# The order of gather jobs in a decoder step: the keys of tile 8 interleaved with the second half of tile 0's values, the keys of tile 5 with the values of tile 8

## The chip, the cores and the metric

The kernel runs on one core of a Trainium2 chip. The metric is the device time of one execution in microseconds (us). The engines are named as in the profile: PE (matmul), PEld (the weight load of a matmul), DVE, ACT, POOL and SP. DMAs are issued from the queues of SP, ACT and POOL.

## The reference, cut to what matters

One decoder layer is computed for 1024 prompt positions and 64 sample positions: a gating and a retention block with a common input and output projection, a cross-attention, and a mixer that picks single-neuron experts. The change touches only the mixer:

```python
def block(xt):                                   # 128 positions
    q = (xt @ wq).reshape(PEER_BLOCK, PEER_HEADS, 2, PEER_DHALF)
    s = jnp.einsum('thcd,hckd->thck', q, subkeys).astype(jnp.float32)
    sv, si = lax.top_k(s, PEER_TOPK)
    ...
    eidx = jnp.take_along_axis(cidx, fi, axis=-1)      # 8 heads x 16 experts a position
    g = jax.nn.softmax(fv, axis=-1).astype(xt.dtype)
    act = jax.nn.gelu(jnp.einsum('thed,td->the', u_tab[eidx], xt))
    return jnp.einsum('the,thed->td', g * act, v_tab[eidx])
```

`u_tab` holds the experts' keys and `v_tab` their values, 16384 rows of 1024 numbers each. A position needs 128 rows of either.

## The kernel before, in words

The 1088 positions are nine tiles: 0 to 7 of 128 rows, and tile 8, the 64 sample rows. They pass through the projections in four batches ([0], [1, 2, 8], [3, 4, 5], [6, 7]). The generator `front` emits this work: the matmuls with streamed weights (line 148), and behind each of them the small steps of the tile. The last steps of a tile are in `post_peer`: scores (lines 602 to 611), two top-k stages on DVE (617 to 642), and the expert numbers by one-hot products (648 to 668), in which POOL does the product of line 660. What comes out is called the selection of the tile here.

The mixer has two ways. Tiles 1 to 4 (`DT`) take the dense way: the selection is turned into a dense matrix of weights by one-hot matmuls (lines 691 to 723; line 691 starts a tile, line 719 is the bulk, one tile at a time), and after `front` the generator `dense` multiplies with all 16384 experts: line 973 with the keys, line 1024 with the values. Tiles 0, 8, 5, 6 and 7 (`GT`) take the gather way, emitted by the generator `gathers`. A gather job fetches 128 rows, 512 KB, by one indirect DMA that POOL issues:

- a `u` job (keys, line 1154) ends in a dot product on DVE (line 1087, called a dot below; two rows in an order or two records in the trace, the second reads the sum out);
- a `v` job (values, line 1157) ends in four narrow matmuls on PE (line 1128; two column halves, each two records in the trace); they are issued for four `v` jobs together, when the fourth has landed, so up to three landed `v` jobs hold their buffers;
- a `w` job (values of tile 7, line 1154 too) ends in a multiply-add on DVE (line 1099).

All jobs share `NG` = 7 buffers `gbuf`, and use a job three jobs after its gather. The jobs stand in one list, made at lines 880 to 892 from `JORD`: parts in one string, parted by a blank, are interleaved by their lengths; "a" and "b" are the halves of a part. A job whose tile has no selection yet holds up the whole list (line 1145). Which instruction of the two generators comes first on an engine is decided at build time by priorities (lines 1163 to 1176, one job costs 1.1 or 1.4 units) and a scheduler; on the chip each engine runs its own list in order.

Of the kernel before, what the change touches and what calls it, by code (L numbers as in the profile page):

```python
# [68 lines left out]
ND = 2  # L69
GT = [0,8,5,6,7]  # L70
DT = [1,2,3,4]
JORD = ("u0","v0","u8","v8","u5","v5a","u6 v5b","u7 v6","w7")
FB = 2
COST_G = 1.4
COST_F = 1.1
# [83 lines left out]
def body(ctx: ExitStack, tc: tile.TileContext, a):  # L159
# [720 lines left out]
    jobs = []  # L880
    for grp in JORD:
        parts = []
# [355 lines left out]
```

## Time and profile before

| | us |
|---|---|
| median of 3 executions | 3674.6 |
| lowest, highest | 3663.38, 3684.58 |
| the profiled execution | 3672.27 |
| its span, first to last instruction | 3670.5 |

The profile is of one execution. A table of stretches gives the busy time of each engine between two times from the span's start, with the count of records behind it, then the granted PE clock as a share of 2.4 GHz, the busy share of the 16 DMA engines and their GB/s. A row of a table of waits reads: the waiting engine, tile and line, what it waited for, total us, times, longest. The profile has 40 slices, each of 91.8 us.

### The profile page before, as it was taken

How to read it: one execution, taken by the hardware profiler on the slowest of the kernel's cores; microseconds unless marked ns; L12 is line 12 of the kernel's file. 1: busy time of each engine (PE TensorE's matmuls, PEld its weight loads, DVE VectorE, ACT ScalarE, POOL GpSimd, SP SyncE). 2: the span in 40 equal slices, each digit the busy share in tenths (PEclk: the TensorE clock that was granted, in tenths of full speed). 3: DMA queues.
4: the chain of work that ended last, by engine and by line, in shares of the span. 5: the costliest groups of instructions: out<-in, count | busy, mean ns of one | idle time of the engine just before them, and what ended most of it. 6: DMA issues, size and time to landing. Idle time of an engine off the chain costs nothing.

```text
span 3670.5 us, 41634 instructions
## 1 busy us (share of the span) xinstructions
PE 3244.9 (88%) x13368; PEld 2037.7 (56%) x13368; DVE 2496.5 (68%) x5941; ACT 1274.3 (35%) x2634; POOL 1784.9 (49%) x1427
## 2 busy tenths in 40 slices
PE   8999558889997899984789779999999999999998
PEld 3444223333445554442445467777777777788886
DVE  2135874325678622799858769878877777799996
ACT  1121211112238785231677932222322322322222
POOL 0013575234546633446744546555565655566631
PEclk9989679899998899986889889999999999999999
DMA  8747677778768887667888879988999989898872
GB/s 271 258 158 275 214 285 278 253 268 283 269 235 330 309 307 283 210 235 263 300 308 313 305 275 338 327 306 316 337 332 347 343 317 324 298 322 318 309 239 75
DMA packets 407354, 1039.67 MB, mean 283 GB/s; under 512 B 37280, under 2 KB 129632, under 8 KB 403040
## 3 DMA queue, kind: packets, MB, share of 16 engines
q0 software_dynamic: 165888, 604.05, 45.3%
q1 hardware_dynamic: 229392, 420.06, 33.5%
q10 hardware_dynamic: 11856, 12.91, 1.0%
q8 instruction: 105, 1.72, 0.2%
q14 instruction: 113, 0.93, 0.1%
HBM read 985.59 MB, written 51.25 MB: 282 GB/s over the span
## 4 chain that ended last, share of the span: by engine, by line
PE 63%; DVE 13%; DMA 9%; POOL 5%; issue 5%; ACT 5%; SPq 0%; POOLq 0%; DVEq 0%; ACTq 0%
PE mm L148 20%; PE h L973 15%; PE cb L1128 5%; PE oa L1024 4%; PE oc L1024 4%; PE od L1024 4%; PE ob L1024 4%; DVE gbuf L1087 4%; DMA gbuf<-in_U_dram,ix 3%; POOL gbuf L1154 2%; PE gb L719 2%; DMA gbuf<-in_V_dram,ixT 2%; DMA ret<-in_cv_dram 1%; ACT oj L702 1%; ACT oj L703 1%
## 5 line engine op out<-in xcount | busy, mean ns | idle before, releaser
L148 PE MATMUL mm<-wr,aT 128*128 128x512 f32 (+1 forms) x2432 | 1126.5, 611 | 34.2 <-DMA aT<-in_xpT_dram 19.0
L1154 POOL DMA_INDIRECT gbuf<-in_U_dram,ix x576 | 711.8, 1236 | 540.7 <-DVE hd L1087 340.2
L1087 DVE CUSTOM_DVE_ANT_0 gbuf<-gbuf,x2g 128x1024 f32<-128x1024 f32 x576 | 733.6, 1287 | 239.7 <-DMA gbuf<-in_U_dram,ix 207.2
L1157 POOL DMA_INDIRECT gbuf<-in_V_dram,ixT x448 | 493.8, 1102 | 568.7 <-PE cb L1128 323.9
L148 PEld LDWEIGHTS mm<-wr,aT 128*128 128x128 f32 (+1 forms) x2432 | 439.2, 190 | 586.0 <-issue 524.2
L973 PE MATMUL h<-x,uh 128*128 128x512 f32 x2048 | 644.3, 392 | 0.8 <-ACT uh L917 0.8
L973 PEld LDWEIGHTS h<-x,uh 128*128 128x128 f32 x2048 | 385.8, 189 | 91.9 <-issue 6.7
L973 PE MATMUL h<-x,ul 128*128 128x512 f32 x1024 | 401.6, 392 | 3.3 <-DVE ul L918 3.3
L917 ACT ACTIVATE vh<-vr 128x1024 fp32r<-128x1024 f32 x128 | 134.9, 1061 | 491.4 <-PE od L1024 487.6
L1128 PE MATMUL cb<-gbuf,Z 128*32 128x512 f32 x1792 | 242.8, 636 | 20.4 <-DMA gbuf<-in_V_dram,ixT 20.3
L1154 POOL DMA_INDIRECT gbuf<-in_V_dram,ix x128 | 182.4, 1425 | 123.6 <-DVE fo L1099 97.8
L917 ACT ACTIVATE ah<-ga 128x512 fp32r<-128x512 f32 x128 | 80.8, 632 | 454.4 <-DVE ga L980 438.7
L719 PE MATMUL gb<-oi,oj 128*128 128x128 f32 x1024 | 168.8, 312 | 68.7 <-ACT big L720 37.9
L918 POOL TENSOR_TENSOR vl<-vr,vh 128x1024 fp32r<-128x1024 f32 x64 | 159.9, 2499 | 130.6 <-ACT vh L917 91.5
L719 PEld LDWEIGHTS gb<-oi,oj 128*128 128x128 f32 x1024 | 151.7, 218 | 127.0 <-ACT oj L703 43.7
L973 PEld LDWEIGHTS h<-x,ul 128*128 128x128 f32 x1024 | 193.0, 188 | 50.0 <-issue 5.0
L703 ACT ACTIVATE oj<-oj,kt 128x128 f32<-128x128 f32 x512 | 215.0, 483 | 0.0
L1099 DVE SCALAR_TENSOR_TENSOR fo<-gbuf,hd,fo 128x1024 f32<-128x1024 f32 x127 | 184.9, 1456 | 1.2
L917 ACT ACTIVATE uh<-ur 128x1024 fp32r<-128x1024 f32 x128 | 134.8, 1054 | 122.5 <-PE h L973 115.7
L705 DVE TENSOR_TENSOR oi<-cst,kt 128x512 f32<-128x512 f32 x128 | 88.9, 700 | 129.4 <-PE gb L719 128.0
L660 POOL TENSOR_TENSOR cd<-cd,sif 128x512 f32<-128x512 f32 (+1 forms) x72 | 105.5, 1478 | 144.4 <-DVE cd L658 134.0
L918 DVE TENSOR_TENSOR ul<-ur,uh 128x1024 fp32r<-128x1024 f32 x128 | 161.8, 1264 | 14.8 <-ACT uh L917 14.7
(232 smaller groups left out, 5102.1 us busy)
## 6 DMA issues: line engine op xcount, KB each, us to landing
ur<-in_Ud_dram SPq DMA_DIRECT2D x128, 512.0 KB, 7.0
vr<-in_V_dram SPq DMA_DIRECT2D x128, 512.0 KB, 5.8
wr<-in_w_in_dram SPq DMA_DIRECT2D x192, 256.0 KB, 5.2
wr<-in_pq_dram SPq DMA_DIRECT2D x128, 256.0 KB, 5.4
gsc<-big SPq DMA_DIRECT2D x32, 1024.0 KB, 6.9
G<-gsc SPq DMA_DIRECT2D x32, 1024.0 KB, 17.9
wr<-in_w_o_dram SPq DMA_DIRECT2D x64, 256.0 KB, 4.9
wr<-in_wq_dram SPq DMA_DIRECT2D x64, 256.0 KB, 6.4
```

The source lines that it names most:

```text
L148: self.nc.tensor.matmul(p, lhsT=lT(k), rhs=w, start=k == 0, stop=k == KB - 1)
L703: nc.scalar.activation(oj[:, r % 4, :], oj[:, r % 4, :], AF.Relu, bias=kt[:, 2, r:r + 1], scale=kt[:, 4, r:r + 1])
L719: nc.tensor.matmul(g4[:, r * 128:(r + 1) * 128], lhsT=oj[:, r, :], rhs=oi[:, r, :], start=True, stop=True)
L917: nc.scalar.activation(hi, raw, AF.Copy)
L918: eng.tensor_tensor(lo, raw, hi.bitcast(F32), op=ALU.subtract)
L973: nc.tensor.matmul(p, lhsT=w[:, k, :], rhs=x[:, k, :], start=k == 0 and j == 0, stop=k == 7 and j == 2)
L1024: nc.tensor.matmul(o[j], lhsT=A[i][ia][:, n * 128:(n + 1) * 128], rhs=Vw[i][iv][:, j * 512:(j + 1) * 512], start=b == 0 and ia + iv == 0, ...
L1087: dot = nc.vector.tensor_tensor_reduce(out=g, in0=g, in1=x2s[t], scale=1.0, scalar=0.0, op0=ALU.mult, op1=ALU.add, accum_out=hd[t][:, i:i ...
L1099: dot = nc.vector.scalar_tensor_tensor(fo[t], g, hd[t][:, i:i + 1], fo[t], op0=ALU.mult, op1=ALU.add)
L1128: nc.tensor.matmul(comb[t][q:q + 32, :], lhsT=Z[:, z + 4 * c1 + r1 % 4, 31 - r1:63 - r1], rhs=g1[:, n * 512:(n + 1) * 512], start=r1 == VQ ...
L1154: nc.gpsimd.indirect_dma_start(out=g, out_offset=None, in_=a["U" if kind == "u" else "V"], in_offset=bass.IndirectOffsetOnAxis(ap=done["ix ...
L1157: nc.gpsimd.indirect_dma_start(out=g, out_offset=None, in_=a["V"], in_offset=bass.IndirectOffsetOnAxis(ap=done["ixT", t][:, i:i + 1], axis=0))
```

## The change

One line is changed. It orders the gather jobs; nothing is computed in another way, and the number of jobs is the same.

```diff
-JORD = ("u0","v0","u8","v8","u5","v5a","u6 v5b","u7 v6","w7")
+JORD = ("u0","v0a","u8 v0b","u5 v8","v5a","u6 v5b","u7 v6","w7")
```

Before, the list has 64 more `v` jobs of tile 0 ahead of the first job of tile 8, and all 64 `v` jobs of tile 8 ahead of the first of tile 5. Now the 64 second `v` jobs of tile 0 alternate with the 64 `u` jobs of tile 8, and of the 128 `u` jobs of tile 5 two go with one `v` job of tile 8. From "v5a" on the list is the same.

**POOL, ahead of tile 8's first gather.** These rows stand where the selections of tiles 1, 2 and 8 are worked out; `cd` is the one-hot product of line 660, `mv` the norm statistics. Before:

```order
L1157 DMA gbuf<-in_V_dram,ixT 128x1024 x7
L660 TENSOR_TENSOR cd<-cd,sif 128x512 x2
L1157 DMA gbuf<-in_V_dram,ixT 128x1024 x4
L660 TENSOR_TENSOR cd<-cd,sif 128x512 x2
L283 TENSOR_TENSOR mv_g<-mv_g,mhalf 128x1 x2
```

After:

```order
L1157 DMA gbuf<-in_V_dram,ixT 128x1024
L283 TENSOR_TENSOR mv_g<-mv_g,mhalf 128x1 x4
L283 TENSOR_TENSOR mv_r<-mv_r,mhalf 128x1 x2
L660 TENSOR_TENSOR cd<-cd,sif 128x512 x2
L283 TENSOR_TENSOR mv_g<-mv_g,mhalf 128x1 x2
L660 TENSOR_TENSOR cd<-cd,sif 128x512 x2
L660 TENSOR_TENSOR cd<-cd,sif 64x512 x2
```

The gathers of tile 0's second half have left this place; they come after the selection of tile 8.

**DVE, in the work on the 14th selection part of the dense tiles (tiles 3 and 4), which goes on beside tile 5's jobs.** `abf` and `ab` belong to the selection. Before:

```order
L650 CAST abf_10143<-ab_10138 128x128
L1087 ISA gbuf_10135,hd_9323<-gbuf_10135,x2g_9249 128x1024
L1087 ISA hd_9323 128x1
L393 TENSOR_TENSOR on_10986<-on_10986,gl_10431 128x128
L1087 ISA gbuf_10186,hd_9323<-gbuf_10186,x2g_9249 128x1024
L1087 ISA hd_9323 128x1
L1087 ISA gbuf_10219,hd_9323<-gbuf_10219,x2g_9249 128x1024
L1087 ISA hd_9323 128x1
L651 SCALAR_TENSOR_TENSOR abf_10143<-abf_10143 128x32
```

After:

```order
L1121 COPY Z_135<-wT_9056 128x8
L341 TENSOR_TENSOR ret_10537<-ret_10537,rt_10542 128x2x64 x2
L650 CAST abf_9874<-ab_9869 128x128
L651 SCALAR_TENSOR_TENSOR abf_9874<-abf_9874 128x32
L1087 ISA gbuf_9917,hd_9029<-gbuf_9917,x2g_8952 128x1024
L1087 ISA hd_9029 128x1
L652 SCALAR_TENSOR_TENSOR abf_9874<-abf_9874 128x32
```

Fewer dots stand between two steps of the selection.

**PE, just ahead of the first one-hot matmul of tile 3.** `nat` are transposes of a normed tile, `mm` the projections. Before:

```order
L296 MATMUL sm<-cst,nat 128x128 x3
L148 MATMUL mm<-wr,aT 128x512 x5
L296 MATMUL sm<-cst,nat 128x128
L148 MATMUL mm<-wr,aT 128x512 x19
L691 MATMUL gb<-cst,eid 128x128 x2
```

After:

```order
L1128 MATMUL cb<-gbuf,Z 32x512 x8
L296 MATMUL sm<-cst,nat 128x128 x4
L148 MATMUL mm<-wr,aT 128x512 x22
L1128 MATMUL cb<-gbuf,Z 32x512 x8
L148 MATMUL mm<-wr,aT 128x512 x6
L691 MATMUL gb<-cst,eid 128x128 x2
```

Groups of eight narrow matmuls of tile 8's `v` jobs now stand among the projections.

Counted over the whole lists: ahead of the first one-hot matmul of tile 3, DVE has 76 dots of tile 5 before and 57 after, and 27 other instructions fewer. When the selections of tiles 6 and 7 are done (the second pair of line 729), PE has behind it 520 narrow matmuls of line 1128 before and 456 after, of 896, with the same 96 of line 973; DVE has done 12 dots of tile 6 before, and none after. The last `w` step stands on DVE where PE's list has 2825 of 3072 matmuls of line 1024 before, and 2976 after.

## Rows read from the trace of the kernel before

**Rows 1.** The profile's page: busy time of the engines, and three lines of the table of 40 slices (tenths).

```profile
PE 3244.9 (88%) x13368; PEld 2037.7 (56%) x13368; DVE 2496.5 (68%) x5941; ACT 1274.3 (35%) x2634; POOL 1784.9 (49%) x1427
...
PE   8999558889997899984789779999999999999998
...
DVE  2135874325678622799858769878877777799996
...
PEclk9989679899998899986889889999999999999999
```

**Rows 2.** Busy time by stretch, all engines: start and end, length, then busy us (records) of PE, PEld, DVE, ACT and POOL, granted clock, DMA share, GB/s.

```profile
900.00:1110.00 210.00, 197.20 (x809) 87.52 (x801) 146.97 (x754) 72.54 (x191) 108.44 (x107) 0.98 0.73 251
1110.00:1450.00 340.00, 298.99 (x1364) 176.11 (x1365) 171.93 (x322) 268.49 (x654) 172.47 (x150) 0.91 0.88 325
1450.00:1520.00 70.00, 70.00 (x219) 33.64 (x218) 43.73 (x228) 20.20 (x53) 8.49 (x9) 1.00 0.43 128
1520.00:1760.00 240.00, 150.16 (x459) 80.40 (x458) 222.43 (x831) 54.42 (x140) 138.27 (x117) 0.78 0.72 252
1760.00:2130.00 370.00, 300.79 (x1391) 183.21 (x1391) 255.71 (x828) 290.73 (x729) 191.07 (x160) 0.88 0.84 305
2570.00:3190.00 620.00, 613.71 (x2888) 454.23 (x2887) 468.68 (x706) 164.36 (x209) 361.19 (x285) 1.00 0.91 327
3190.00:3550.00 360.00, 360.00 (x1565) 293.71 (x1564) 356.27 (x411) 107.80 (x136) 219.99 (x143) 1.00 0.89 313
```

**Rows 3.** Busy time by stretch of line 1128 alone (PE, PEld), the narrow matmuls of the `v` jobs.

```profile
900.00:1110.00 210.00, 38.23 (x300) 7.96 (x292) 0.98 0.73 251
2570.00:3190.00 620.00, 65.18 (x528) 14.01 (x528) 1.00 0.91 327
```

**Rows 4.** Waits in the stretch 900 to 1110 us: the longest of POOL, and the first of the selection's chain.

```profile
POOL gbuf L1157 <- PE cb L1128: 56.5, 16, 8.9
...
ACT sif L626 <- DVE si L622: 24.7, 6, 6.0
```

**Rows 5.** The first gathers of tile 8 on POOL, from the timeline (start us, us).

```profile
1114.48 1.01 POOL L1154 DMA_INDIRECT gbuf<-in_U_dram,ix  x1 [4.71 <-DMA ix<-ix]
```

**Rows 6.** Busy time by stretch of line 1087 alone (DVE), the dots.

```profile
1520.00:1760.00 240.00, 97.82 (x153) 0.78 0.72 252
```

**Rows 7.** The timeline of PE around the start of tile 3's one-hot matmuls, and at the end of tile 4's (start us, us; in brackets the idle time before, and what ended it).

```profile
1753.61 0.69 PE L691 MATMUL gb<-cst,eid 128*128 128x128 f32 x2 [25.96 <-DVE eid L664]
...
2125.69 2.75 PE L719 MATMUL gb<-oi,oj 128*128 128x128 f32 x10 [1.04 <-ACT oj L703]
```

**Rows 8.** Waits of DVE for the gathers of keys, and the gathers of keys issued (count, us to landing): first the stretch 1520 to 1870 us, in which tile 5's `u` jobs run alone, then 2210 to 2570 us, in which `u6` and `v5b` run two to one.

```profile
DVE gbuf L1087 <- DMA gbuf<-in_U_dram,ix: 13.8, 10, 5.4
...
gbuf<-in_U_dram,ix POOLq DMA_INDIRECT x128, 6.7
...
DVE gbuf L1087 <- DMA gbuf<-in_U_dram,ix: 46.9, 33, 6.0
...
gbuf<-in_U_dram,ix POOLq DMA_INDIRECT x96, 7.4
```

**Rows 9.** The longest wait of POOL in the stretch 1760 to 2130 us.

```profile
POOL gbuf L1157 <- PE cb L1128: 77.3, 17, 12.5
```

**Rows 10.** DVE at the end of the `w` jobs and tile 7's last steps, from the timeline (start us, us).

```profile
3552.61 2.59 DVE L1099 SCALAR_TENSOR_TENSOR fo<-gbuf,hd,fo 128x1024 f32<-128x1024 f32 x2
3555.24 1.23 DVE L1070 SCALAR_TENSOR_TENSOR gbuf<-gbuf,fo 128x1024 f32<-128x1024 f32 x1
3556.50 1.28 DVE L276 BATCH_NORM_STATS2 bn_y<-gbuf 128x6 f32<-128x512 f32 x2
...
3565.39 1.23 DVE L898 TENSOR_TENSOR gbuf<-gbuf 128x1024 f32<-128x1024 f32 x1 [0.44 <-ACT gbuf L288]
...
3567.66 1.22 DVE L899 TENSOR_TENSOR gbuf<-gbuf 128x1024 f32<-128x1024 f32 x1
```

**Rows 11.** Busy time by stretch of POOL's gather issues alone: line 1157 in the first row, line 1154 in the other two.

```profile
900.00:1110.00 210.00, 68.42 (x69) 0.98 0.73 251
...
1520.00:1760.00 240.00, 98.97 (x82) 0.78 0.72 252
...
3190.00:3550.00 360.00, 179.17 (x126) 1.00 0.89 313
```

**Rows 12.** The last matmul of PE, from the timeline (start us, us).

```profile
3652.52 0.40 PE L1024 MATMUL od<-vh,al 128*128 128x512 f32 x1
```

## The prediction, made before the changed kernel ran

> **What bounds the kernel now.** I read the page first, then busy time by stretch, then the waits and the timeline inside the stretches that the change touches. From slice 24 on (2,200 us) PE is busy nine tenths or more nearly everywhere [rows 1]: the dense part is bound by PE, and whatever PE has to do there costs its full time. Before that PE has holes. The stretches show them [rows 2]. In 900 to 1110 us (tile 0's second half of `v` jobs) PE is busy 197.2 of 210 us. In 1110 to 1450 us (`u8`, then `v8`) it stands still for 41 of 340 us. In 1520 to 1760 us (tile 5's `u` jobs) PE is busy only 150.2 of 240 us, while DVE has 222.4: there DVE sets the pace, and PE then waits 26 us for a selection on DVE [rows 7]. In 1760 to 2130 us PE, ACT and DVE have 301, 291 and 256 of 370 us, and none is full. So the question for the change is where PE's `v` work goes (out of a stretch full on PE, or into one), and how many dots stand ahead of the selections on DVE.
>
> **The change part by part.** All work stays the same in sum; I follow PE's and DVE's lists from stretch to stretch. Gains are negative.
>
> *900 to 1110 us: 64 `v` jobs leave.* In the changed list nothing of the gathers is left here but the end of "v0a". A job is four records of line 1128, and a record takes 38.23 / 300 = 0.127 us [rows 3], so 64 x 4 x 0.127 = 32.6 us of PE. PE is busy 94% here, so I take 0.94 x 32.6 = -30.6. POOL also loses the waits for these buffers, 56.5 us [rows 4], behind which the selection's product of line 660 stood. What is late next: tile 8's first gather still waits for its selection [rows 5], a chain over DVE, ACT and POOL, and DVE is 147 of 210 us busy [rows 2]. If that chain sets the end of the stretch, the gain is 0; so the bounds are -33 and 0.
>
> *1110 to 1450 us: the same 64 `u` and 64 `v` jobs, mixed.* The `v` jobs are now tile 0's. Before, DVE is loaded in the first half and PE in the second; mixed, PE's 41 us of standing still could fall to the share of the stretch before (6%): 299 / 0.94 = 318, or -22. Nothing shows how much of the idle time came from the dots, so I take half, -11, with bounds -22 and +11.
>
> *1450 to 1520 us* has no gather in either list: 0.
>
> *1520 to 1760 us: `u5` with `v8`.* Up to the first one-hot matmul of tile 3, DVE has 57 dots in place of 76, and 27 other instructions fewer. A dot takes 97.82 / 76.5 = 1.28 us (two records each) [rows 6]; the others (222.43 - 97.82) / (831 - 153) = 0.18 us [rows 2, 6]. That is 19 x 1.28 + 27 x 0.18 = 29.3 us less on the engine that sets the pace: -29.3. PE takes up some 28 `v` jobs, 28 x 4 x 0.127 = 14 us, in its 90 us of idle time: 0. But each dot now depends on a queue that PE can hold up. Up to three `v` jobs hold their buffers until the fourth lands, so a gather of keys starts later, and DVE, in order, waits for it with the selection behind. The row that is nearest is the stretch in which `u6` and `v5b` run two to one: 46.9 us of waits for 96 dots, 0.49 us a dot, against 13.8 / 128 = 0.11 with `u5` alone [rows 8]. The difference over 57 dots is 57 x 0.38 = +21.7. The bounds are 0 (the dots there come 0.7 as often, with more time for each) and the price of the slower rival below, +73.
>
> *1760 to 2130 us: one-hot matmuls of tiles 3 and 4, the last projections.* The lists of both kernels have the same 256 one-hot matmuls, the same projections and nearly the same `v` jobs between these two points, 136 narrow matmuls before and 144 after; 71 dots of tile 5 stand here in place of 52, but the 12 of tile 6 have left. I take 0, with bounds of 15 to either side.
>
> *Dense part: more `v` work in it.* At the same place of the lists PE is 64 narrow matmuls behind (520 against 456), which are 32 jobs. They are paid where PE is full, at 65.18 / 132 = 0.494 us a job [rows 3]: +15.8. Without that the gain in 900 to 1110 us would be counted twice.
>
> *The end.* The list's end comes later against PE's: after the last `w` step 96 matmuls of line 1024 are left, where 247 were. 360 us of `w` jobs with DVE at 99% [rows 2] move along with PE and slow it no more than before. Tile 7's last steps, 1.23 + 1.28 + 1.23 + 1.22 = 5.0 us on DVE [rows 10], now fall among PE's last accumulations: +5, with bounds 0 and +15 (DVE late by several steps as well).
>
> The sum is -30.6 - 11 - 29.3 + 21.7 + 15.8 + 5 = -28.4. Against the profiled execution, 3672.3 us with a span of 3670.5, that gives 3643.9. The median of the three executions is 2.3 us above the profiled one, so I put the forecast at 3646 us, 0.8% faster.
>
> **The rivals.**
>
> *Larger gain.* Dots find their gathers landed (DMA engines are 72% busy in 1520 to 1760 us, and 90% where I took the wait from), mixing gives all of the 22 us, and the end costs nothing: -30.6 - 22 - 29.3 + 15.8 = -66, or 3608 us. For it: DVE waited only 10 times for `u5`'s gathers [rows 8]. Against it: there were seven free buffers then.
>
> *No change.* PE's 30.6 us in 900 to 1110 us don't come back, since tile 8's selection sets the end of the stretch: 3646 + 31 = 3677 us. For it: ACT waits 24.7 us for the top-k on DVE there [rows 4], so the chain is not far behind. Against it: PE was 94% busy.
>
> *Slower.* In 1520 to 1760 us buffers of `v` jobs come free only when PE gets to their narrow matmuls, and PE's list has these behind transposes and projections that themselves wait for DVE. POOL then waits, and gathers of keys, line 660 and the norms queue behind it. POOL's waits for line 1128 cost 77.3 / 17 = 4.5 us each where `v` jobs stand among one-hot work [rows 9]; 16 groups of four `v8` jobs make 73 us in place of my 21.7, and mixing gives nothing: 3646 + 51 + 11 = 3708 us. It turns the sign when DVE's waits for gathers of keys, from the first `u5` job to tile 3's first one-hot matmul, pass some 50 us. For it: PE stood still for 90 us there, each time behind something. Against it: with PE so free, a narrow matmul seldom has other matmuls ahead of it.
>
> *POOL's issue blocked.* An issue takes 0.99 us where DVE is 70% busy, 1.21 us where it is 93%, and 1.42 us at 99% [rows 2, 11]: it gets longer beside a busy DVE, and the change puts 28 issues more into the 93% stretch. If each of the 85 issues there had to wait for a whole dot, POOL would have 138 + 34 + 85 x 1.28 = 281 us in a stretch of 240, and be the bound: +41, or 3687 us. The rows speak against it, with 0.2 us longer and not 1.28. The Trainium skill ("SBUF — State Buffer", section "SBUF: two separate sides") states such a lock: while DVE runs an operation that takes the port pair it shares with GpSimd, GpSimd can't write a DMA's descriptors. By that rule the sum would be this rival's.
>
> That the change does nothing is excluded: POOL's list shows the gathers moved.
>
> **How the numbers follow.** Forecast 3646 us (its own range 3631 to 3661): 0.47. Larger gain, about 3608: 0.18. No change, about 3677: 0.15. Slower, about 3708: 0.17. Blocked issue, about 3687: 0.03. A difference under 0.5% (18.4 us) can't be told from none, so "same" is 3656 to 3693. Faster: most of the forecast and the larger gain, 0.61. Same: the rest of the forecast, most of no change, 0.21. Slower: 0.18. For 8 in 10 I go from 3604 to 3692: it leaves out the far half of the slower cases and the best end of the larger gain.
>
> **What would show it.** Right: the first gather of tile 8 starts some 30 us before 1114 us; PE is at 95% or more up to it; tile 3's first one-hot matmul comes 40 to 60 us before 1753.6, and tile 4's last at about 2085 in place of 2128; DVE's wait for gathers of keys between is 20 to 35 us; the last `w` step ends within 40 us of PE's last matmul. Wrong: tile 8's first gather stays near 1110 (no change); DVE's waits in the `u5` stretch grow beyond 50 us, or POOL's waits for line 1128 beside `u5` reach 70 us (slower); the time from PE's last matmul to the end of the span grows well beyond the 17 us of before [rows 12] (the end).

## The result, and the profile after

The changed kernel takes 3725.8 us (median; 3718.1 to 3732.5), the kernel before 3677.6 us beside it: a ratio of 1.0135, with a 95% interval of 1.0097 to 1.0174. It is slower by 1.3%, above the end of the range (3604 to 3692 us), where 0.8% faster was forecast. The profiled execution has a span of 3719.6 us, 49.1 us longer than before.

The page's busy times of the engines, and the line of the dots, after. To be read against [rows 1]: PE's and DVE's busy shares are the same 88% and 68%. For the same 13368 matmul records PE is busy 30.7 us longer, and 18.4 us of the longer span are idle time of PE. On DVE 324.4 us of idle time ahead of dots end in a gather of keys (207.2 us in the page of before).

```profile
PE 3275.6 (88%) x13368; PEld 2044.7 (55%) x13368; DVE 2512.0 (68%) x5941; ACT 1277.1 (34%) x2636; POOL 1763.9 (47%) x1427
...
L1087 DVE CUSTOM_DVE_ANT_0 gbuf<-gbuf,x2g 128x1024 f32<-128x1024 f32 x576 | 743.9, 1301 | 375.4 <-DMA gbuf<-in_U_dram,ix 324.4
```

Busy time by stretch, after; the columns are those of [rows 2].

```profile
900.00:1110.00 210.00, 178.04 (x584) 88.05 (x584) 154.51 (x791) 77.82 (x217) 45.63 (x44) 0.92 0.31 103
1110.00:1450.00 340.00, 299.56 (x1342) 175.04 (x1342) 163.46 (x303) 257.36 (x629) 153.46 (x145) 0.93 0.85 307
1520.00:1760.00 240.00, 176.38 (x613) 87.17 (x611) 218.42 (x848) 73.12 (x190) 147.10 (x134) 0.84 0.86 300
1760.00:2130.00 370.00, 290.94 (x1329) 174.00 (x1329) 253.22 (x786) 267.49 (x663) 183.50 (x158) 0.87 0.83 295
```

In 900 to 1110 us PE has 19 us less to do, and yet tile 8's first gather hardly moves (1110.16 us, [rows 5]: 1114.48). In 1520 to 1760 us PE is busy 26 us more, and yet tile 3's first one-hot matmul comes at 1732.43 us, 21 us earlier than in [rows 7]. Then the gain is lost: the last group of tile 4's one-hot matmuls starts at 2143.00 us ([rows 7]: 2125.69), its last matmul at 2146.1 (2128.0). Timelines of POOL and PE, after:

```profile
1110.16 1.20 POOL L1154 DMA_INDIRECT gbuf<-in_U_dram,ix  x1 [5.20 <-PE gb L719]
...
1732.43 0.38 PE L691 MATMUL gb<-cst,eid 128*128 128x128 f32 x2
...
2143.00 3.48 PE L719 MATMUL gb<-oi,oj 128*128 128x128 f32 x16 [3.04 <-ACT big L720]
...
3701.68 0.39 PE L1024 MATMUL od<-vh,al 128*128 128x512 f32 x1
```

The path from start to end, cut at these milestones, holds the whole difference:

| from ... to | before, us | after, us | forecast | measured |
|---|---|---|---|---|
| start to tile 8's first gather | 1114.5 | 1110.2 | -30.6 | -4.3 |
| to tile 5's first part of the selection (line 668) | 407.8 | 410.3 | -11 | +2.5 |
| to tile 3's first one-hot matmul | 231.3 | 211.9 | -29.3 + 21.7 | -19.4 |
| to tile 4's last one-hot matmul | 374.4 | 413.7 | 0 | +39.3 |
| to the first matmul of line 1024 | 14.0 | 24.3 | 0 | +10.3 |
| dense part, to the last matmul | 1510.5 | 1531.3 | +15.8 | +20.8 |
| to the end of the span | 18.0 | 17.9 | +5 | -0.1 |
| sum | | | -28.4 | +49.1 |

What rises beside the 39.3 us, the table of waits shows. DVE's waits for gathers of keys, after, in 1110 to 1520, 1520 to 1740 and 1740 to 2150 us:

```profile
DVE gbuf L1087 <- DMA gbuf<-in_U_dram,ix: 86.9, 29, 7.0
...
DVE gbuf L1087 <- DMA gbuf<-in_U_dram,ix: 8.8, 10, 1.8
...
DVE gbuf L1087 <- DMA gbuf<-in_U_dram,ix: 56.3, 25, 6.4
```

Before, the same three are 4.4, 4.7 and 15.9 us. Both new mixed stages have them: the first stretch is that of tile 8's keys with tile 0's values, the last that of tile 5's with tile 8's, beside one-hot matmuls.

A wait on DVE costs time only where something else waits for it. Between tile 3's first and tile 4's last one-hot matmul PE is busy 302.3 us before and 310.7 after, so 30.8 of the 39.3 us are idle time of PE (72.1 and 102.9 us). Two of PE's waits grow by as much, for gathers of values and for one-hots that DVE makes; others rise and fall. In 1740 to 2150 us, before and then after:

```profile
PE cb L1128 <- DMA gbuf<-in_V_dram,ixT: 4.5, 1, 4.5
PE gb L719 <- DVE oi L705: 3.6, 1, 3.6
...
PE cb L1128 <- DMA gbuf<-in_V_dram,ixT: 19.6, 9, 6.5
PE gb L719 <- DVE oi L705: 19.3, 4, 7.5
```

The timeline of 1776 to 1803 us, after, shows one such wait from the inside (POOL, then DVE, then PE):

```profile
1779.94 0.93 POOL L1157 DMA_INDIRECT gbuf<-in_V_dram,ixT  x1 [0.30 <-issue]
1785.41 1.79 POOL L1154 DMA_INDIRECT gbuf<-in_U_dram,ix  x1 [4.54 <-DVE hd L1087]
...
1794.35 1.15 POOL L1157 DMA_INDIRECT gbuf<-in_V_dram,ixT  x1 [5.90 <-DVE hd L1087]
...
1783.91 1.22 DVE L1087 CUSTOM_DVE_ANT_0 gbuf<-gbuf,x2g 128x1024 f32<-128x1024 f32 x1 [0.83 <-DMA gbuf<-in_U_dram,ix]
...
1785.17 1.23 DVE L1087 CUSTOM_DVE_ANT_0 gbuf<-gbuf,x2g 128x1024 f32<-128x1024 f32 x1
...
1792.84 1.23 DVE L1087 CUSTOM_DVE_ANT_0 gbuf<-gbuf,x2g 128x1024 f32<-128x1024 f32 x1 [6.44 <-DMA gbuf<-in_U_dram,ix]
...
1789.05 1.95 PE L719 MATMUL gb<-oi,oj 128*128 128x128 f32 x16
1790.93 1.92 PE L1128 MATMUL cb<-gbuf,Z 128*32 128x512 f32 x16
```

Counted in the timeline up to 1785.4 us, POOL has issued 164 gathers of values and PE has taken 160: four of the seven buffers hold values, the last of them issued at 1779.94, and PE comes to them at 1790.93, after one-hot matmuls. POOL waits 4.54 us until the dot of 1783.91 frees one, issues a key at 1785.41, and that key's dot starts at 1792.84 after DVE has stood still for 6.44 us. The dot waits for the gather, and the gather for the dot before.

### The profile page after: what moved, and what is told of

It reads as the page before. It is cut to its first block, busy times and chain, and to the rows that moved or that the text cites. A ratio compares the mean times of both kernels' runs of the same rounds, so it can differ in the third digit from the quotient of the medians.

```text
span 3719.6 us, 41714 instructions
## 1 busy us (share of the span) xinstructions
PE 3275.6 (88%) x13368; PEld 2044.7 (55%) x13368; DVE 2512.0 (68%) x5941; ACT 1277.1 (34%) x2636; POOL 1763.9 (47%) x1427
## 5 line engine op out<-in xcount | busy, mean ns | idle before, releaser
L1087 DVE CUSTOM_DVE_ANT_0 gbuf<-gbuf,x2g 128x1024 f32<-128x1024 f32 x576 | 743.9, 1301 | 375.4 <-DMA gbuf<-in_U_dram,ix 324.4
L1154 POOL DMA_INDIRECT gbuf<-in_U_dram,ix x576 | 684.7, 1189 | 644.0 <-DVE hd L1087 380.3
L1128 PE MATMUL cb<-gbuf,Z 128*32 128x512 f32 x1792 | 251.2, 657 | 44.3 <-DMA gbuf<-in_V_dram,ixT 43.7
L702 ACT ACTIVATE oj<-cst,kt 128x128 f32<-128x128 f32 x512 | 162.1, 389 | 19.4 <-PE gb L719 17.7
```

Of the source, the lines that this page charges most:

```text
L702: nc.scalar.activation(oj[:, r % 4, :], iota, AF.Abs, bias=kt[:, 3, r:r + 1])
L1087: dot = nc.vector.tensor_tensor_reduce(out=g, in0=g, in1=x2s[t], scale=1.0, scalar=0.0, op0=ALU.mult, op1=ALU.add, accum_out=hd[t][:, i:i ...
L1128: nc.tensor.matmul(comb[t][q:q + 32, :], lhsT=Z[:, z + 4 * c1 + r1 % 4, 31 - r1:63 - r1], rhs=g1[:, n * 512:(n + 1) * 512], start=r1 == VQ ...
L1154: nc.gpsimd.indirect_dma_start(out=g, out_offset=None, in_=a["U" if kind == "u" else "V"], in_offset=bass.IndirectOffsetOnAxis(ap=done["ix ...
```

## The experiments

The theory: a group of four value gathers, spread among keys, keeps up to four of the seven buffers from the keys until PE has read them; key gathers then start late, DVE waits, and its selections, PE's work that hangs on them, and undone jobs move back. The rivals: the loss comes with the values put off at tile 0; or only the order of the dots counts. Each kernel's instruction lists are built anew by the scheduler, so every edit also alters the lists a little; how much that alone can cost is taken up at the end of this section.

Differences between kernels below are taken from the ratios to the kernel before, times its 3677 us. Waits and milestones are of the profiled executions.

| kernel | median us | ratio to before (95%) | DVE's key waits 1110-1520 | 1740-2150 | first matmul of line 1024 | dense part |
|---|---|---|---|---|---|---|
| before | 3677.6 | | 4.4 | 15.9 | 2142.0 | 1510.5 |
| changed | 3725.8 | 1.0135 (1.0097 to 1.0174) | 86.9 | 56.3 | 2170.4 | 1531.3 |
| E1 first part alone | 3669.2 | 0.9985 (0.9973 to 0.9997) | 72.7 | 1.3 | 2108.0 | 1532.4 |
| E2 second part alone | 3684.5 | 1.0029 (1.0016 to 1.0041) | 7.6 | 50.6 | 2123.6 | 1534.4 |
| E3 changed, VQ=2 | 3661.0 | 0.9964 (0.9951 to 0.9977) | 47.6 | 17.3 | 2122.4 | 1520.1 |
| E4 before, VQ=2 | 3692.9 | 1.0051 (1.0039 to 1.0064) | 5.8 | 4.3 | 2169.7 | 1508.5 |
| E5 changed, runs of four beside tile 5 | 3692.0 | 1.0053 (1.0033 to 1.0074) | 77.9 | 24.9 | 2129.0 | 1543.0 |
| E6 changed, NG=8, NR=7 | 3702.9 | 1.0078 (1.0059 to 1.0097) | 60.5 | 17.1 | 2172.0 | 1520.8 |
| E7 changed, NR=7 | 3740.0 | 1.0174 (1.0154 to 1.0193) | 70.6 | 52.7 | 2175.1 | 1542.5 |
| E8 second part, VQ=2 | 3666.7 | 0.9979 (0.9966 to 0.9993) | 7.1 | 20.1 | 2123.0 | 1520.0 |
| E9 nothing mixed | 3651.8 | 0.9942 (0.9927 to 0.9958) | 16.1 | 7.7 | 2113.3 | 1515.4 |
| E10 changed, all in runs of four | 3701.4 | 1.0072 (1.0059 to 1.0086) | 40.4 | 26.4 | 2144.9 | 1537.5 |
| E11 changed, VQ=2, runs of two | 3655.8 | 0.9949 (0.9936 to 0.9962) | 52.4 | 14.6 | 2116.1 | 1522.9 |
| E14 first stage taken apart | 3691.6 | 1.0054 (1.0034 to 1.0073) | 13.7 | 48.1 | 2110.9 | 1533.6 |

**E1 and E2, either part alone.**

```diff
-JORD = ("u0","v0a","u8 v0b","u5 v8","v5a", ...
+JORD = ("u0","v0a","u8 v0b","v8","u5","v5a", ...     # E1
+JORD = ("u0","v0","u8","u5 v8","v5a", ...            # E2
```

> Only the first part of the change: keys of tile 8 mixed with the second half of tile 0's values, then tile 8's values alone, then tile 5's keys alone. Theory 1 (buffers: values of tile 8 beside keys of tile 5 hold the gather buffers until TensorE reads them, so keys come late and VectorE waits with the selections behind): a small loss only, from PE's narrow matmuls that move into the dense part, +5 to +20 us (3683 to 3698), and VectorE waits for keys in 1520 to 2130 us at 10 to 25 us. Rival (the loss is carried by the values that are put off at the first tile, and ends in the dense part whatever runs beside tile 5's keys): +35 to +55 us (3713 to 3733), with the waits unchanged at about 14 us.

> Only the second part of the change: tile 0's values and tile 8's keys one after the other as in the kernel before, then tile 5's keys mixed with tile 8's values. Theory 1 (buffers): nearly the whole loss, +35 to +55 us (3713 to 3733), with VectorE's waits for keys from tile 5's first to the selections of tiles 6 and 7 above 50 us. Rival (the loss comes with the first part): within 15 us of the kernel before (3663 to 3693). Rival (only the order of the dots against the selections): the loss is there, but VectorE's waits for keys stay under 25 us.

Neither part alone carries the loss, so the theory in its first form and the first rival both fall: E1 is 0.15% faster than before, and E2 only 0.3% slower, though its waits of 50.6 us are those that were expected. The waits come and go with the mixed stages; the time does not yet.

**E3 and E4, groups of two values in place of four.**

```diff
-VQ = 4
+VQ = 2
```

> The changed kernel with the narrow matmuls of the values issued for two gathers together in place of four (VQ=2), so that values hold at most one buffer while the group fills, and nothing else is altered. Theory 1 (buffers): VectorE's waits for keys in 1740 to 2150 us fall from 56 us to 20 to 30 us, and the time to 3680 to 3705 us. Rival (order of the dots): the waits and the time stay, 3715 to 3735 us. Half groups may cost PE something by themselves; the same edit on the kernel before shows how much.

> The kernel before with VQ=2, to show what groups of two cost or bring without the change. Theory 1 (buffers): the last three pairs of stages (keys of 6 with values of 5, keys of 7 with values of 6) are mixed here too and VectorE waits 46.9 us in them, so a little is gained or nothing, 3655 to 3685 us. Rival (order of the dots): no difference, 3670 to 3685 us.

The changed kernel gains 63 us, more than was expected, and is now faster than the kernel before. The order of the jobs is the same, so the order of the jobs alone is not the cause. From the end of tile 5's selection to tile 6's first part it takes 164.4 us (1769.5 to 1933.8) in place of 199.9 (1779.0 to 1978.9). The waits of DVE in just these stretches, of the changed kernel:

```profile
DVE gbuf L1087 <- DMA gbuf<-in_U_dram,ix: 49.2, 22, 6.4
```

and of E3:

```profile
DVE gbuf L1087 <- DMA gbuf<-in_U_dram,ix: 13.4, 12, 2.1
```

35.8 us less of waiting, 35.5 us less of time. That the two agree is no proof: in this stretch PE is busy 149.0 us in place of 169.3, which is 20 of the 35 us. And 15 of the 63 us stand already at tile 8's first gather (1095.4 us), ahead of any mixed stage, though only 7 are left at tile 5's first part. The kernel before loses 19 us by the same edit, against both expectations; tile 8's first gather comes at 1134.7 there (1114.5), and what made it later was not looked into. So VQ=2 is no gain by itself; it pays where keys and values are mixed.

**E5, the changed order with the values in runs.** Eight keys, then four values, in the stage of tile 5 only; VQ and NG as they were.

```diff
-        n = max(len(p) for p in parts)
+        n = max(len(p) for p in parts) // (8 if grp == "u5 v8" else 1)
```

> The changed kernel with tile 5's keys and tile 8's values in the same stage, but eight keys in a row, then four values in a row, in place of two keys and one value; the instruction lists are otherwise nearly the same as in the changed kernel, with groups of four (VQ=4) and seven buffers. Four values in a row land together, so no landed value holds a buffer for the time of several dots. Theory 1 (buffers held by half-full groups): VectorE's waits for keys in 1740 to 2150 us fall from 56 us to 15 to 35 us, and the time by 20 to 45 us, to 3680 to 3705 us. Rival (fewer, smaller matmul groups are what helped with VQ=2, or only the order of the dots counts): waits and time stay, 3710 to 3735 us.

Until tile 5's selection is done it agrees with the changed kernel to 2 us (1777.1 against 1779.0). The waits that follow halve, in E5

```profile
DVE gbuf L1087 <- DMA gbuf<-in_U_dram,ix: 24.9, 16, 4.7
```

in 1740 to 2150 us, and the dense part starts 41 us earlier. The time falls by 30 us. Neither the size of PE's groups nor the amount of work differs. How long a part-filled group stands does, and so, a little, does the place of dots and matmuls in the lists. The dense part is 12 us longer than in the changed kernel; it gives part of the gain back.

**E6 and E7, one buffer more, and its control.** Eight buffers need room, which a shorter ring of streamed weights gives; E7 has that ring and seven buffers.

```diff
-NR = 9
-NG = 7
+NR = 7
+NG = 8        # E6; E7 keeps 7
```

> The changed kernel with eight gather buffers in place of seven; the memory for it comes from the ring of streamed weights, which falls from nine to seven tiles. Theory 1 (buffers): against the changed kernel with that ring of seven and seven gather buffers, the waits of VectorE for keys in 1740 to 2150 us fall by 15 to 40 us and the time by 10 to 35 us. Rival (buffers don't matter, only how values are grouped on PE does): no difference to that kernel beyond 8 us.

> The control for the kernel with eight buffers: the changed kernel with the ring of streamed weights of seven tiles and seven gather buffers. Both theories: near the changed kernel, 3715 to 3760 us, with VectorE's waits for keys in 1740 to 2150 us at 45 to 70 us.

One buffer is worth 35 us (1.0174 to 1.0078), and the waits in 1740 to 2150 us fall from 52.7 to 17.1. Between the two profiled executions it is 28 us (E6's is 10 us above its median). But the dense part starts only 3 us earlier; 22 of these 28 us are in the dense part itself (1542.5 to 1520.8). From the end of tile 5's selection to tile 6's first part it is 175 us in both (1817.5 to 1992.5, 1830.0 to 2005.0). Waits of DVE in this stretch, in E6:

```profile
DVE oi L705 <- PE gb L719: 38.4, 15, 6.3
...
DVE gbuf L1087 <- DMA gbuf<-in_U_dram,ix: 12.3, 8, 2.8
```

E7 has 16.9 and 43.1 us there. DVE waits for PE's one-hot matmuls instead. The lists differ too: PE's has 48 records of line 1128 fewer left for the dense part (864 against 912). So a wait on DVE is not worth its length in every kernel.

**E8, E10 and E11, three more mixes.** E8 is E2 with VQ=2; E10 and E11 put all mixed stages in runs, of four with VQ=4 and of two with VQ=2.

```diff
-        n = max(len(p) for p in parts)
+        n = min(len(p) for p in parts) // 4     # E10; E11: // 2
```

> The second part of the change alone (tile 5's keys mixed with tile 8's values, 3684 us measured, with 60 us of waits for keys) with groups of two values (VQ=2). Theory 1 (buffers): the waits for keys fall to 15 to 30 us and the time by 15 to 40 us, to 3645 to 3670 us. Rival (the gain of VQ=2 in the changed kernel comes from the first part's mixed stage): 3680 to 3695 us.

> The changed kernel with all mixed stages in runs of four values (tile 8's keys with tile 0's values, tile 5's with tile 8's, and the two mixed stages in the dense part). By the buffer theory it is no slower than the kernel in which only the stage of tile 5's keys was put in runs (3692 us measured): 3670 to 3695 us, with the dense part, 1543 us there, at 1515 to 1540 us. Rival (VectorE's waits in the dense part cost nothing, since PE bounds it): 3685 to 3700 us, dense part unchanged.

> A candidate: the changed kernel with VQ=2 (3661 us measured) and all mixed stages in runs of two values, so that a group's gathers follow one another directly. By the buffer theory the waits for keys in 1740 to 2150 us fall from 17 us to 10 us or less, and the time is 3645 to 3662 us. Rival (with 17 us of waits there is no more to get): 3655 to 3670 us.

E8 came out as the theory had it: waits of 20.1 us, 18 us less time. E10 missed its range and its rival's: the waits in 1110 to 1520 us fell only to 40.4, the dense part is 1537.5 us, and it is no faster than E5 (7 us slower, with intervals that overlap); runs of four are no general cure. E11 is faster than before by 0.5%, but its waits are 14.6 us and not the 10 that were expected, and its time lies in both ranges, so it can't tell its theory from its rival.

**E9 and E14, one stage or both taken apart.**

```diff
-JORD = ("u0","v0a","u8 v0b","u5 v8","v5a", ...
+JORD = ("u0","v0a","u8","v0b","v8","u5","v5a", ...   # E9
+JORD = ("u0","v0a","u8","v0b","u5 v8","v5a", ...     # E14
```

> The second values of tile 0 only put off behind tile 8's keys, with no stage of the first part and none of the second mixed: u8, then v0b, v8, u5 one after the other. It takes the mixing out of 1110 to 1520 us. Theory of the prediction (mixing fills PE's holes there): from tile 8's first gather to tile 5's first selection it takes 10 to 20 us longer than the 411 us of the changed kernel. Rival (nothing is gained by mixing, PE or the chain of the projections sets the length): within 8 us of 411. In all, by the buffer theory, no waits for keys beside tile 5 (under 25 us in 1520 to 2150 us) and 3665 to 3700 us.

> The changed kernel with only its first mixed stage taken apart (u8, then v0b, then tile 5's keys with tile 8's values). It stands between the changed kernel (3726 us) and the one without either mixed stage (3652 us). Buffer theory: tile 8's keys no longer wait (87 us of waits in 1110 to 1520 us fall below 30), tile 5's still do (45 us or more in 1740 to 2150 us); 3680 to 3710 us. Rival (the loss belongs to the pair of mixed stages, and either alone costs nothing): 3650 to 3670 us.

With E1 and the changed kernel these make a square (medians, us):

| ratio to before | tile 5's keys, tile 8's values apart | mixed |
|---|---|---|
| tile 8's keys, tile 0's values apart | 0.9942 (E9) | 1.0054 (E14) |
| mixed | 0.9985 (E1) | 1.0135 (changed) |

The first mixing costs 16 or 30 us, the second 41 or 55, both together 71. What the change does besides, putting 64 values of tile 0 behind tile 8's keys, is worth 21 us in E9: E9 is the fastest kernel of all, 0.6% below the kernel before, and below the range that was expected of it. E2 lost little for a like reason: without values between tile 8's first gather and tile 5's selection, that stretch takes 378 us (1125.1 to 1503.0) in place of 408. E9 also settles the stretch from tile 8's first gather to tile 5's selection: 396.9 us (401.0 in E14), against 410.3 with the first stage mixed. Both expectations missed that, for both had no loss by mixing. In E14 the second mixing shows in another place: the dense part starts where it does in E9 (2110.9 and 2113.3), but takes 18 us longer, and PE's last matmul is at 3644.52 us

```profile
3644.52 0.40 PE L1024 MATMUL od<-vh,al 128*128 128x512 f32 x1
```

of a span of 3684.4: 39.9 us before the end, where E9 has 18.3. Its last `w` gather starts at 3650.4 us, behind that matmul, so the `w` jobs end the kernel.

**E12 and E13, the stretch 900 to 1110 us.** Less work on DVE alone, in the kernel before (E12) and in the changed one (E13):

```diff
-            nc.vector.match_replace(x, sv[:P, j, 0:8], x, NEG)
-            nc.vector.max(sv[:P, j, 8:16], x)
-            nc.vector.max_index(si[:P, j, 8:16], sv[:P, j, 8:16], x)
+            nc.vector.tensor_copy(sv[:P, j, 8:16], sv[:P, j, 0:8]) if t in (1, 2) else nc.vector.match_replace(x, sv[:P, j, 0:8], x, NEG)
+            nc.vector.tensor_copy(si[:P, j, 8:16], si[:P, j, 0:8]) if t in (1, 2) else nc.vector.max(sv[:P, j, 8:16], x)
+            t in (1, 2) or nc.vector.max_index(si[:P, j, 8:16], sv[:P, j, 8:16], x)
```

> The kernel before, with the second eight candidates of the first top-k of tiles 1 and 2 left out (three top-k instructions replaced by two copies, 32 times, some 20 to 24 us of VectorE's work by their mean times, nearly all of it in 900 to 1110 us; tiles 1 and 2 get other weights). PE has the same work in that stretch, the 64 value jobs included. Theory of the prediction (PE, busy 94%, sets the end of the stretch): tile 8's first gather stays within 5 us of 1114.5. Rival (the chain of the selections sets it): the first gather comes 10 to 24 us earlier, at 1090 to 1105.

> The same edit (the second eight candidates of the first top-k of tiles 1 and 2 left out) on the changed kernel, in which the 64 value jobs are gone from 900 to 1110 us and PE is busy some 85%. In the kernel before it took 10.5 us from VectorE there and moved tile 8's first gather by only 0.9 us. Theory (with the value jobs gone, the chain over the engines that ends in tile 8's selection sets the stretch): the first gather comes 5 to 15 us before the changed kernel's 1110.2. Rival (PE's own list still sets it, and the value jobs were never on the path): within 3 us.

The edit took only 10.5 us from DVE in this stretch in E12, not 20 to 24. The stretch and the first gather of tile 8, in E12:

```profile
900.00:1110.00 210.00, 198.43 (x819) 87.48 (x817) 136.46 (x696) 75.53 (x198) 105.79 (x107) 0.98 0.74 255
...
1113.63 1.01 POOL L1154 DMA_INDIRECT gbuf<-in_U_dram,ix  x1 [6.89 <-PE sm L384]
```

and in E13:

```profile
900.00:1110.00 210.00, 179.15 (x614) 94.54 (x606) 139.44 (x701) 89.83 (x241) 51.51 (x52) 0.91 0.33 108
...
1097.43 1.02 POOL L1154 DMA_INDIRECT gbuf<-in_U_dram,ix  x1 [7.34 <-PE sm L384]
```

Before, with PE full, the gather moves by 0.9 us; after the change, with the values gone, by 12.7 us (1110.16 to 1097.43) for 15 us less on DVE. But the two don't decide between their theories. The first top-k that the edit shortens (line 617 of tile 1) starts 4.7 us later in E12 than before (863.3 and 858.6), and 5.6 us earlier in E13 than in the changed kernel (860.7 and 866.3); from that point to the gather the edit gives 5.5 us in E12 and 7.1 in E13, nearly the same. E3 has its first gather at 1095.4 us with none of this work left out. What shows that the selection comes last is a wait of PE for the last step of tile 8's selection, just ahead of the gather, before (906 to 1112 us) and after (900 to 1110):

```profile
PE gb L729 <- DVE eid L666: 2.5, 1, 2.5
...
PE gb L729 <- DVE eid L666: 9.8, 1, 9.8
```

So at this point the selection was the last already before the change, with PE hardly ahead of it. How much PE's own work slows the selection, whose chain passes PE too, these runs don't separate.

**What these runs leave untested.** In all, E12 took 3692.7 us and E13 3675.9, in one run each, with the kernel before at 3671.0 and 3673.7 beside them. So with less work on DVE the kernel before is 22 us slower, and the changed kernel 47 us faster. E13 keeps the key waits, 55.6 us in 1740 to 2150 us, and yet needs 610.4 us from tile 5's first part to the first matmul of line 1024, where the changed kernel needs 649.9 and the kernel before 619.8. E2, E7 and E14 have 48 to 53 us of key waits as well, and take 620.6, 611.5 and 603.4 us; with 8 to 26 us of them (E3, E5, E6, E8 to E11) it is 602 to 623 us. So the key waits by themselves don't set this stretch, and part of what E3, E5 and E6 gave back may be owed to the lists as they were built anew. No run keeps every engine's list and frees the buffers alone.

## Why the prediction was wrong, by its own steps

**The step that failed most: "1760 to 2130 us: 0 (±15)".** It measured +39.3, of which 30.8 are idle time of PE. The prediction counted equal work on both sides and priced no waits there. It had a mechanism for them, values that hold buffers, but charged it to 1520 to 1760 us alone, at +21.7. In 1520 to 1740 us the waits rose by only 4.1 us (4.7 to 8.8), and that step gained 19.4 where 7.6 was forecast. The waits came 200 us later, 40.4 us more of them on DVE in 1740 to 2150 us, and on PE 15.1 us more for gathers of values and 15.7 more for DVE's one-hots. The half of tile 5's keys that stands behind that point had been counted as dots, not as gathers in need of buffers. That the waits stand in this stretch is shown; that they alone make its length is not, since E2, E7, E13 and E14 have the key waits without it. What made PE wait longer here than in those kernels stays open.

**The form of the rival "slower".** It was nearest, 3708 us for 3726, but by luck: it put the loss into 1520 to 1760 us, and its signs, 50 us of key waits or 70 us of POOL's waits for line 1128 beside `u5`, did not come there (8.8 us, and next to none). The longest waits of POOL in 1740 to 2150 us, after:

```profile
POOL gbuf L1157 <- PE cb L1128: 39.9, 11, 11.1
POOL gbuf L1154 <- DVE hd L1087: 38.6, 16, 4.9
POOL gbuf L1154 <- PE cb L1128: 22.5, 2, 12.9
POOL gbuf L1157 <- DVE hd L1087: 18.2, 9, 5.9
```

62.4 us are for line 1128, where it was 84.7 before (77.3 of them in [rows 9]), and 56.8 us for a dot, where it was 29.5. So POOL's waits for PE fell, and what grew are its waits for dots: the keys turn round in the few buffers that are left. With smaller groups, runs or one buffer more (E3, E5, E6) DVE's key waits fall to 17 to 25 us.

**"-30.6" for 900 to 1110 us** gave 4.3. That PE's work comes back in full was wrong: tile 8's selection was already the last, and PE's wait for it grew from 2.5 to 9.8 us. The rival "no change" had said so, and its sign came (first gather near 1110). PE's busy time fell by only 19.2 us although 30.2 us of narrow matmuls left ([rows 3]: 38.23 us), its idle time rose by as much, 12.8 to 32.0 us, and the granted clock of the stretch fell from 0.98 to 0.92. Line 1128 alone in 900 to 1110 us, after:

```profile
900.00:1110.00 210.00, 8.06 (x48) 1.41 (x48) 0.92 0.31 103
```

**"-11" for mixing in 1110 to 1450 us** measured +2.5, and against the same order without mixing 410.3 - 396.9 = 13 us too long. The forecast asked how PE's holes would fill and left out that tile 8's keys share the buffers as well: 86.9 us of waits in place of 4.4. DVE has slack there, 163 of 340 us busy, so most of them can have cost little.

**The dense part, +15.8,** measured +20.8. The narrow matmuls there went from 92.1 to 103.6 us, +11.5 (24 jobs more, not 32: 96 records); the rest is not traced to one cause. The +10.3 just ahead of it were put at nothing: 32 records of line 1128 stand there after the change, and none before. **The end, +5,** was 0.

**Blocked issue** did not happen at that size: POOL is busy 147.1 us of 240 in 1520 to 1760 us, not the 281 of that rival, and an issue takes 109.44 / 102 = 1.07 us in the mean. Single issues were held up, though. In the timeline above, the issue at 1779.94, beside no dot, takes 0.93 us; the one at 1785.41 begins inside the dot of 1785.17, takes 1.79 us and ends 0.8 us after that dot. Of the 102 issues only 19 begin inside a dot (1.43 us in the mean; the other 83 take 0.99). The rival had every issue meet a whole dot. By the lock that the Trainium skill states (page "SBUF — State Buffer", section "SBUF: two separate sides") an issue that meets an operation of DVE on the shared port pair has to wait for its end; the trace agrees for these issues.

**What stays open:** why E10's runs of four in the first stage make tile 5's selection come 20 us later than in the changed kernel (1540.6 and 1520.5), why VQ=2 costs the kernel before 19 us, and 9 us of the dense part. That interleaving costs 71 us in these four kernels is shown by the square. That it does so by holding buffers is the reading that E3, E5 and E6 against E7 favour, for the second stage; it is not closed, since E12 and E13 moved by 22 and 47 us with the buffers left as they were. For the first stage only the waits (86.9 us, 13.7 when taken apart) and the 16 and 30 us speak for it, as no run altered its groups alone.

## What to carry to other kernels

When two kinds of jobs share a pool of buffers, ask of each kind how long a buffer is held after its data has landed, and how many are then left for the other kind. Where a job is used only in groups, smaller groups, or a group's transfers next to each other, are worth a trial; here they gave back 63 and 30 us, but not in every kernel (E4, E10). A wait of this kind has to be looked for over the whole life of the mixed stage, and priced on the engine that sets the pace: the same 50 us of waits on DVE went with a stretch 30 us longer in one kernel, and with none in four others. And a change of order is often two changes: here, moving work behind another's start was worth 21 us, and interleaving it cost 71.

## What the runs showed that was not expected

Mixing keys and values lowers no count of instructions and no transfer, and DMA was not the limit: in the stretch between tile 5's and tile 6's selections the changed kernel moved 312 GB/s with the DMA engines 87% busy, E3 352 GB/s at 94%. So the DMA engines could have carried more than they were given there.
